# Row halves taken in turn for a state-space mixer's outputs, and four sums of squares that leave for four column quarters together

## The chip, the cores and the metric

The kernel runs on one core of a Trainium2 chip. The metric is the device time of one launch in microseconds (us), as the median of several runs. The kernel before has three: 2160.73, 2167.41 and 2173.29 us, so its median is 2167.41 us.

## The reference, cut to what matters

A trunk of two layers works on 1024 tokens of 1024 channels, in float32. The change lies in layer 0, whose mixer has two branches:

```python
# even_mixer
proj = rms_norm(h, ln) @ w_in
u = proj[..., :512]                         # S5 block: 32 groups of 16 channels
q, k, v = split(proj[..., 512:], 3)         # attention: 8 heads of 64
q = rms_norm(to_heads(q), q_gain)           # mean of 64 squares for each head
k = rms_norm(to_heads(k), k_gain)
# s5_mixer: for each group a complex diagonal recurrence over 64 states
y = einsum(x_r, c_re) - einsum(x_i, c_im) + d * u
y = gelu(y); y = y * sigmoid(y @ w_glu)
```

After it stand stick-breaking attention, an output projection, a squared-ReLU MLP and a gated embedding; layer 1 has a pooling mixer in place of S5 and attention. None of that is touched.

## The kernel before, in words

Activations lie with channels on the 128 partitions and tokens along the free axis, in two halves (`hf`) of 512 tokens. Large products (`gemm`, L477) split both operands into a high and a low part and run three matmuls for each 128 channels. The smaller products of S5, of the norms and of the scores take float32 operands as they are: the trace shows two MATMUL records for each such matmul, and one for each matmul of `gemm`.

**The generators.** `build` writes the work as Python generators, which `weave` interleaves at given rates. Keys, values and queries of a token half come from `kvq`; the four passes of S5 (`s5_pass`, eight of the 32 groups each) are woven into them. What the generators emit is then put into one fixed order for each engine by the framework's scheduler, so a small change in the text can move instructions of other steps too.

**One S5 pass.** Tables of powers are built on DVE and POOL (L319 to L321, L301 to L306). A short product gives the kernel's first taps (L352), which 16 small DMAs lay out as the matrix M (L364). The inputs are transposed (L378, L387) into U. Products of U with VT (L396), whose outputs take the two column halves in turn, give the scan's input. DVE and POOL rotate, scan and rotate back (L400, L408), which yields the states X with real and imaginary part `ri`; the group of an even index has its 64 states on partitions 0 to 63, that of an odd index on 64 to 127. Then come the outputs, the first place of the change: for each group one matmul of U with M over all 128 partitions (L426) and two of X with `ca` over 64 partitions (L428), summed in the same part of a PSUM tile `py`. The four even groups go first, ACT copies their tile out (L431), then the four odd ones. L437 transposes the result back.

**The norms of q and k.** `proj` makes four tiles of 128 channels, two heads each, for a token half, and calls `put_qk` with `j` from 0 to 3. DVE scales the tile (L636), ACT squares it into `sq` (L637), and PE sums the squares of each head with a narrow matmul by `sel` (L638) into rows `32*j` to `32*j+31` of the tile `st`. That is the second place of the change: it comes 16 times, four for each of k and q in each token half. After the fourth, `rsqrt` (L505 to L510, ACT and DVE) makes the reciprocal norms, ACT and DVE split them (L644, L645), four matmuls (L648, the tile `b`) spread them over the heads' rows, and DVE applies them (L650).

**Buffers.** `sq` comes from the tag `t2` (three buffers), which `rsqrt` and `put_v` use too; `acc` (two buffers) holds the input norm's sums and later the two parts at L644. PSUM has two banks each for `z`, `mm` and `b`, one each for `av` and `st`.

Of the kernel before, what the change touches and what calls it, by code (L numbers as in the profile page):

```python
# [19 lines left out]
P = 128  # L20
SEQ = 1024
HT = 512
# [18 lines left out]
class Kern:  # L41
# [282 lines left out]
    def s5_pass(self, gt):  # L324

        nc = self.nc
        v, g = nc.vector, nc.gpsimd
# [12 lines left out]
        ca = self.s5_prod(gt, C2, CS, 0, "ca", g)  # L340
# [5 lines left out]
        for g2 in range(2):  # L346
            rows = slice(64 * g2, 64 * g2 + 64)
            g.tensor_copy(out=self.BD[rows, :, :, 16 * g2:16 * g2 + 16], in_=B2[rows])
        pk = self.p([P, 4, P], "z")
        for m in range(4):  # L350
            for ri in range(2):
                nc.tensor.matmul(pk[0:32, m], self.BD[:, m, ri, :], ca[:, 2 * m + ri].rearrange("p j h -> p (j h)"),  # L352
                                 start=(ri == 0), stop=(ri == 1))
# [5 lines left out]
        M = self.a([P, 8, P], "M")  # L359
# [23 lines left out]
        U = self.a([P, 8, P], "U")  # L383
# [8 lines left out]
        for ri in range(2):  # L392
            pv = self.p([P, 4, P], "z")
            for gl in range(8):
                m, g2 = gl // 2, gl % 2
                nc.tensor.matmul(pv[64 * g2:64 * g2 + 64, m], VT[:, 2 * m + ri, 64 * g2:64 * g2 + 64], U[:, gl],  # L396
                                 start=True, stop=True)
# [13 lines left out]
        X = self.a([P, 2, 4, P], "X")  # L411
        g.memset(X[:, :, :, 0:1], 0.0)
        n = P - 1
        for ri in range(2):
# [3 lines left out]
            tt(v, o, o, b, ALU.subtract if ri == 0 else ALU.add)  # L418
            yield
        yT = self.t([P, 8, 8, 16], "wq", name="yT")  # L420
        for g2 in range(2):
            py = self.p([P, 4, P], "z")
            rows = slice(64 * g2, 64 * g2 + 64)
            for m in range(4):
                gl = 2 * m + g2
                nc.tensor.matmul(py[:, m], U[:, gl], M[:, gl], start=True, stop=False)  # L426
                for ri in range(2):
                    nc.tensor.matmul(py[:, m], X[rows, ri, m, :],  # L428
                                     ca[rows, 2 * m + ri].rearrange("p j h -> p (j h)"),
                                     start=False, stop=(ri == 1))  # L430
            nc.scalar.copy(out=yT[:, :, g2::2, :].rearrange("p t g h -> p g t h"),  # L431
                           in_=py.rearrange("p g (t h) -> p g t h", h=16))
        yield
        for hb in range(2):
            pt = self.p([P, 4, P], "z")
# [193 lines left out]
    def put_qk(self, which, hf, j, ps):  # L629

        nc, v = self.nc, self.nc.vector
        if j == 0:
            self.st = self.p([P, HT], "st")
        sq = self.t([P, HT], "t2", name="sq")
        d = self.qk_dst(which, hf, j)
        v.tensor_tensor(out=d, in0=ps, in1=self.r[hf], op=ALU.mult)  # L636
        nc.scalar.activation(out=sq, in_=d, func=AF.Square)  # L637
        nc.tensor.matmul(self.st[32 * j:32 * j + 32], self.sel, sq, start=True, stop=True)  # L638
        if j == 3:
            r = self.t([P, HT], "t2", name="rq")  # L640
            self.rsqrt(self.st, 64.0, r)

            hi, r4 = (self.t([P, HT], "acc", F32R, name="rq") for _ in range(2))
            nc.scalar.copy(out=hi, in_=r)  # L644
            v.scalar_tensor_tensor(out=r4, in0=hi.bitcast(F32), scalar=self.gain[:, 59:60], in1=r, op0=ALU.mult, op1=ALU.subtract)  # L645
            for i in range(4):
                pb = self.p([P, HT], "b")
                nc.tensor.matmul(pb, self.selT[32 * i:32 * i + 4], r4[32 * i:32 * i + 4], start=True, stop=True)  # L648
                d = self.qk_dst(which, hf, i)
                v.scalar_tensor_tensor(out=d, in0=d, scalar=self.qg[:, which:which + 1], in1=pb, op0=ALU.mult, op1=ALU.mult)  # L650
# [830 lines left out]
```

## Time and profile before

| What | Value |
|---|---|
| Median of three runs | 2167.41 us |
| The profiled execution's own time | 2161.73 us |
| Its span, first to last instruction | 2159.9 us |
| PE busy in the span | 2072.2 us (96%) |
| DVE / ACT / POOL busy | 1838.9 / 1142.2 / 132.1 us |
| Mean granted TensorE clock | 0.98 |
| Projections and S5 | about 0 to 262 us |
| Attention, alone or woven with others | about 262 to 620 us |
| The MLPs, embeddings and pooling | from there to the end |

PE is the engine for matmuls, PEld its weight loads, DVE, ACT and POOL the vector, scalar and general engines. A duration in the table of groups is that of one record from its start to its modelled end. Records on PE overlap, since one starts while the one before it drains, so the time that PE spends on a step is read from start to start in the timeline, and not from durations. The value in brackets behind a row of the timeline is the engine's idle time before it and what ended that.

### The profile page before, as it was taken

The page shows a single profiled execution, that of the slowest core. Times are in us where ns is not written, and L with a number is a line of the kernel's source. Part 1 is how long each engine was busy: PE and PEld are TensorE (multiplying, and loading weights), DVE is VectorE, ACT ScalarE, POOL GpSimd, SP SyncE. Part 2 cuts the span into 40 slices and gives each one's busy share as a digit, 9 for nine tenths or more (in the row PEclk, how much of TensorE's full clock was granted, in tenths as well). Part 3 has the DMA queues.
Part 4 walks back from the last instruction along what each step waited for, and adds up shares of the span by engine and source line. Part 5 has one row for each costly group of instructions (what it writes and reads, how often), then busy time and mean ns, then how long its engine had stood idle before and what let it go on. Part 6 is the DMA issues. An engine that isn't in the chain of part 4 may idle for free.

```text
span 2159.9 us, 24772 instructions
## 1 busy us (share of the span) xinstructions
PE 2072.2 (96%) x9464; PEld 1624.3 (75%) x9464; DVE 1838.9 (85%) x2443; ACT 1142.2 (53%) x1613; POOL 132.1 (6%) x263
## 2 busy tenths in 40 slices
PE   7899999989998999999999999888999999999997
PEld 5676766656577888888888887566888888888886
DVE  8866578978879888998878978999697998879998
ACT  5133466756644563756356555533654656365662
POOL 3856000000000000000000000000000000000000
PEclk9998999989899999999999999998999999999999
DMA  4111111220024112102202122322111201211221
GB/s 151 55 55 55 55 49 32 71 83 30 15 76 138 37 59 69 59 30 78 78 8 71 59 88 69 98 77 99 59 48 41 79 33 56 78 54 34 69 69 59
DMA packets 44742, 136.25 MB, mean 63 GB/s; under 512 B 9552, under 2 KB 10704, under 8 KB 44624
## 3 DMA queue, kind: packets, MB, share of 16 engines
q1 hardware_dynamic: 44624, 134.67, 18.6%
q8 instruction: 74, 1.21, 0.2%
q14 instruction: 44, 0.36, 0.1%
HBM read 129.28 MB, written 4.19 MB: 62 GB/s over the span
## 4 chain that ended last, share of the span: by engine, by line
PE 75%; DVE 19%; ACT 3%; issue 2%; DMA 1%; POOL 0%; SPq 0%; DVEq 0%; ACTq 0%
PE mm L477 27%; PE z L477 15%; PE b L477 12%; PE av L477 6%; PE st L477 6%; DVE rz L698 2%; DVE X L863 2%; DVE w L450 2%; PE z L682 1%; PE av L730 1%; PE b L712 1%; PE z L428 1%; DVE xgl L529 1%; DVE acc L499 1%; DVE na L713 1%
## 5 line engine op out<-in xcount | busy, mean ns | idle before, releaser
L477 PE MATMUL mm<-xgh,w 128*128 128x512 f32 x912 | 300.0, 405 | 15.5 <-ACT w L446 6.2
L450 DVE TENSOR_TENSOR w<-q,w 128x1024 fp32r<-128x1024 f32 x204 | 246.8, 1217 | 0.3 <-ACT w L446 0.3
L446 ACT CAST w<-q 128x1024 fp32r<-128x1024 f32 x204 | 212.8, 1047 | 29.0 <-PE mm L477 14.8
L477 PEld LDWEIGHTS mm<-xgh,w 128*128 128x128 f32 x912 | 173.1, 192 | 62.5 <-issue 9.1
L446 ACT CAST hsh<-H 128x1024 fp32r<-128x1024 f32 x98 | 102.3, 1047 | 197.1 <-PE st L477 88.5
L477 PE MATMUL mm<-xgl,w 128*128 128x512 f32 x456 | 183.0, 401 | 0.0
L446 ACT CAST w<-wr 128x1024 fp32r<-128x1024 f32 x98 | 102.3, 1047 | 150.1 <-PE mm L477 97.9
L477 PE MATMUL z<-xsh,w 128*128 128x512 f32 x576 | 177.7, 390 | 0.0
L863 DVE TENSOR_TENSOR q<-q,q 128x1024 f32<-128x1024 f32 x114 | 137.0, 1219 | 14.0 <-DMA q<-in_w_down 9.5
L450 DVE TENSOR_TENSOR w<-wr,w 128x1024 fp32r<-128x1024 f32 x98 | 128.1, 1312 | 21.1 <-ACT w L446 9.7
L477 PE MATMUL mm<-hsh,w 128*128 128x512 f32 x448 | 137.9, 389 | 0.0
L477 PE MATMUL b<-xsh,w 128*128 128x512 f32 x448 | 137.9, 389 | 0.0
L450 DVE TENSOR_TENSOR hsl<-H,hsh 128x1024 fp32r<-128x1024 f32 x98 | 119.4, 1219 | 11.4 <-ACT hsh L446 11.3
L446 ACT CAST xsh<-X 128x1024 fp32r<-128x1024 f32 x72 | 75.6, 1050 | 98.2 <-PE st L477 51.2
L477 PEld LDWEIGHTS z<-xsh,w 128*128 128x128 f32 x576 | 108.1, 188 | 22.9 <-issue 0.5
L477 PE MATMUL mm<-xsh,w 128*128 128x512 f32 x400 | 123.8, 389 | 0.0
L450 DVE TENSOR_TENSOR xsl<-X,xsh 128x1024 fp32r<-128x1024 f32 x72 | 87.4, 1220 | 38.7 <-ACT xsh L446 38.2
L477 PE MATMUL z<-xsl,w 128*128 128x512 f32 x288 | 112.1, 389 | 0.0
L450 DVE TENSOR_TENSOR xsl<-xt,xsh 128x512 fp32r<-128x512 f32 x108 | 70.1, 685 | 42.5 <-ACT xsh L446 42.5
L477 PEld LDWEIGHTS mm<-xgl,w 128*128 128x128 f32 x456 | 87.9, 193 | 21.8 <-issue 4.1
L477 PE MATMUL b<-hsh,w 128*128 128x512 f32 x336 | 103.6, 389 | 0.0
L477 PE MATMUL z<-hsh,w 128*128 128x512 f32 x336 | 103.4, 389 | 0.0
(360 smaller groups left out, 4874.5 us busy)
## 6 DMA issues: line engine op xcount, KB each, us to landing
q<-in_w_up SPq DMA_DIRECT2D x56, 512.0 KB, 3.6
q<-in_w_down SPq DMA_DIRECT2D x56, 512.0 KB, 3.7
wr<-in_w_in SPq DMA_DIRECT2D x26, 512.0 KB, 3.6
wr<-in_w_out SPq DMA_DIRECT2D x16, 512.0 KB, 3.5
wr<-in_w_up SPq DMA_DIRECT2D x16, 512.0 KB, 3.5
wr<-in_w_down SPq DMA_DIRECT2D x16, 512.0 KB, 3.5
x<-in_x SPq DMA_DIRECT2D x15, 512.0 KB, 5.7
wr<-in_w_gate SPq DMA_DIRECT2D x15, 512.0 KB, 3.5
```

What stands on the lines that cost most here:

```text
L428: nc.tensor.matmul(py[:, m], X[rows, ri, m, :], ca[rows, 2 * m + ri].rearrange("p j h -> p (j h)"), start=False, stop=(ri == 1))
L446: nc.scalar.copy(out=hi, in_=src)
L450: e.tensor_tensor(out=lo, in0=src, in1=hi.bitcast(F32), op=ALU.subtract)
L477: self.nc.tensor.matmul(ps, a, b, start=(first and n == 0 and i == 0), stop=(last and n == K - 1 and i == 2), skip_group_check=going)
L499: e.tensor_tensor(out=self.acc[hf], in0=self.acc[hf], in1=sq, op=ALU.add)
L529: self.nc.vector.scalar_tensor_tensor(out=lo, in0=x, scalar=g, in1=hi.bitcast(F32), op0=ALU.mult, op1=ALU.subtract)
L682: nc.tensor.matmul(pz[:, 0:b1 - b0], self.q[hf][pair // 2][rows, pair % 2, i * P:(i + 1) * P], self.k[b0 // HT][pair // 2][rows, pair % 2, ...
L698: v.tensor_tensor_scan(out=rz[:, rev], data0=na[:, rev], data1=rz[:, rev], initial=0.0, op0=ALU.add, op1=ALU.add)
L712: nc.tensor.transpose(pt[:, (kb - k0) * P:(kb - k0 + 1) * P], zs[:, kb * P:(kb + 1) * P], self.ident)
L713: v.tensor_copy(out=wT[:, k0 * P:k1 * P], in_=pt[:, 0:(k1 - k0) * P])
L730: nc.tensor.matmul(self.avp[64 * o:64 * o + 64, i * P:(i + 1) * P], self.v[kb // 4 * 2 + pair // 2][:, kb % 4, cs], w[:, at * P:(at + 1) * ...
L863: (self.nc.vector if eng == "v" else self.nc.gpsimd).tensor_tensor(out=o, in0=a, in1=b, op=op)
```

## The change

Two places change, and the names of lines shift by two to seven (L426 stays L426, L428 becomes L429, L638 becomes L645, L648 becomes L655, L477 becomes L479).

The outputs of S5 now hold two PSUM tiles at once, one for the even and one for the odd groups. For each `m` the two matmuls by M come first, then the four by X, with even and odd groups in turn. Both copies to `yT` stand behind all of them. In `put_qk`, the squares are kept in a list, the first two in the tag `acc` and the last two in `t2`; the tile `st` is taken at the fourth, and all four matmuls by `sel` are written there, one after the other. No product is added or removed.

```diff
-        for g2 in range(2):
-            py = self.p([P, 4, P], "z")
-            rows = slice(64 * g2, 64 * g2 + 64)
-            for m in range(4):
-                gl = 2 * m + g2
-                nc.tensor.matmul(py[:, m], U[:, gl], M[:, gl], start=True, stop=False)
-                for ri in range(2):
-                    nc.tensor.matmul(py[:, m], X[rows, ri, m, :],
-                                     ca[rows, 2 * m + ri].rearrange("p j h -> p (j h)"),
-                                     start=False, stop=(ri == 1))
+        py = [self.p([P, 4, P], "z") for _ in range(2)]
+        rows = [slice(64 * g2, 64 * g2 + 64) for g2 in range(2)]
+        for m in range(4):
+            for g2 in range(2):
+                nc.tensor.matmul(py[g2][:, m], U[:, 2 * m + g2], M[:, 2 * m + g2], start=True, stop=False)
+            for ri in range(2):
+                for g2 in range(2):
+                    nc.tensor.matmul(py[g2][:, m], X[rows[g2], ri, m, :],
+                                     ca[rows[g2], 2 * m + ri].rearrange("p j h -> p (j h)"),
+                                     start=False, stop=(ri == 1))
+        for g2 in range(2):
             nc.scalar.copy(out=yT[:, :, g2::2, :].rearrange("p t g h -> p g t h"),
-                           in_=py.rearrange("p g (t h) -> p g t h", h=16))
+                           in_=py[g2].rearrange("p g (t h) -> p g t h", h=16))
...
         if j == 0:
-            self.st = self.p([P, HT], "st")
-        sq = self.t([P, HT], "t2", name="sq")
+            self.sqs = []
+        sq = self.t([P, HT], ("acc", "acc", "t2", "t2")[j], name="sq")
...
-        nc.tensor.matmul(self.st[32 * j:32 * j + 32], self.sel, sq, start=True, stop=True)
+        self.sqs.append(sq)
+        if j == 3:
+            self.st = self.p([P, HT], "st")
+            for i, sq in enumerate(self.sqs):
+                nc.tensor.matmul(self.st[32 * i:32 * i + 32], self.sel, sq, start=True, stop=True)
```

The built programs show what stands in PE's row. At the start of the first pass's outputs, PE has before (`z_961` is the PSUM tile of the even groups):

```order
L426 MATMUL z_961<-M_747,U_835 128x128
L428 MATMUL z_961<-ca_670,X_952 128x128 x2
L426 MATMUL z_961<-M_747,U_835 128x128
L428 MATMUL z_961<-ca_670,X_952 128x128 x2
L426 MATMUL z_961<-M_747,U_835 128x128
L638 MATMUL st_817<-sq_948,s5blk_378 32x512
L428 MATMUL z_961<-ca_670,X_952 128x128 x2
```

Now PE has at the same place, with `z_957` for the even and `z_958` for the odd groups:

```order
L426 MATMUL z_957<-M_747,U_833 128x128
L426 MATMUL z_958<-M_747,U_833 128x128
L429 MATMUL z_957<-ca_670,X_948 128x128
L429 MATMUL z_958<-ca_670,X_948 128x128
L429 MATMUL z_957<-ca_670,X_948 128x128
L429 MATMUL z_958<-ca_670,X_948 128x128
L426 MATMUL z_957<-M_747,U_833 128x128
```

Matmuls over 64 partitions and over 128 change places once for each two groups where they did once for each group, and the square of k's third tile no longer stands between them.

The squares of q's first token half, ahead of the third pass's outputs, stand so in PE's row now (`mm_1719` is a projection tile of q, `mm_1792` the first tile of the next keys):

```order
L479 MATMUL mm_1719<-xgl_93,w_1653 128x512
L645 MATMUL st_1753<-sq_1474,s5blk_378 32x512
L645 MATMUL st_1753<-sq_1609,s5blk_378 32x512
L645 MATMUL st_1753<-sq_1682,s5blk_378 32x512
L479 MATMUL mm_1792<-xgh_291,w_1721 128x512
L479 MATMUL mm_1792<-xgh_291,w_1722 128x512
L479 MATMUL mm_1792<-xgl_292,w_1721 128x512
L645 MATMUL st_1753<-sq_1750,s5blk_378 32x512
```

Three squares stand side by side, and the scheduler has put three matmuls of a projection ahead of the fourth. In the other three groups it is three and one as well, with other work between them. Before, the four stood 25 to 58 PE instructions apart.

In the third pass's outputs PE has before, around the matmuls that spread q's norms (L648, then L655):

```order
L426 MATMUL z_1829<-M_1562,U_1641 128x128
L638 MATMUL st_1823<-sq_1824,s5blk_378 32x512
L428 MATMUL z_1829<-ca_1485,X_1782 128x128
L648 MATMUL b_1770<-rq_1767,selT 128x512
L648 MATMUL b_1773<-rq_1767,selT 128x512
L428 MATMUL z_1829<-ca_1485,X_1782 128x128
```

And now:

```order
L429 MATMUL z_1828<-ca_1483,X_1782 128x128
L426 MATMUL z_1827<-M_1560,U_1638 128x128
L655 MATMUL b_1770<-rq_1767,selT 128x512
L655 MATMUL b_1773<-rq_1767,selT 128x512
L426 MATMUL z_1828<-M_1560,U_1638 128x128
L429 MATMUL z_1827<-ca_1483,X_1782 128x128
```

Thirteen of the pass's 24 output matmuls stand ahead of the first of these now, and eleven did before; between the last square and it, 21 projection matmuls stand where 17 did, and no square where one did. Behind attention's start the scheduler has put rows of all engines into another order, through 27 of attention's 48 units; PE, DVE and ACT have as many instructions as before.

## The prediction, made before the changed kernel ran

> **What bounds the kernel now.** I read the page first, then the busy times by stretch, then the chain of waits in the stretch where the change lies, and last the timeline of PE there. The page gives the engines' shares and the chain of the whole span:
>
> ```profile
> PE 2072.2 (96%) x9464; PEld 1624.3 (75%) x9464; DVE 1838.9 (85%) x2443; ACT 1142.2 (53%) x1613; POOL 132.1 (6%) x263
> PE 75%; DVE 19%; ACT 3%; issue 2%; DMA 1%; POOL 0%; SPq 0%; DVEq 0%; ACTq 0%
> ```
>
> The changed steps run from about 77 to 331 us. By stretch (busy us of PE, PEld, DVE, ACT and POOL, then PE's clock):
>
> ```profile
> 140.00:180.00 40.00, 38.63 (x203) 29.67 (x202) 24.04 (x28) 12.36 (x19) 29.40 (x58) 1.00 0.17 53
> 180.00:220.00 40.00, 37.96 (x167) 26.85 (x166) 30.34 (x37) 10.71 (x15) 22.32 (x48) 0.83 0.16 53
> 220.00:260.00 40.00, 38.66 (x217) 28.20 (x216) 21.54 (x34) 13.74 (x20) 4.21 (x2) 1.00 0.25 74
> 300.00:340.00 40.00, 37.28 (x192) 23.86 (x191) 32.05 (x49) 25.22 (x43) 0.00 (x0) 1.00 0.16 54
> 345.00:620.00 275.00, 260.38 (x1384) 170.65 (x1385) 244.52 (x319) 177.14 (x260) 0.00 (x0) 0.94 0.13 44
> ```
>
> PE is busy for 95 to 97% of them, and no other engine comes near before attention. In attention DVE has 89% as well. The chain from 60 to 262 us:
>
> ```profile
> by line: PE mm L477 29.3%; PE z L428 10.1%; DVE S L408 5.9%; PE z L426 5.7%; DVE W L400 5.1%; PE z L396 4.1%; PE st L638 3.7%; issue 3.6%; POOL W L400 2.9%; PE z L352 2.8%; DVE s5blk L211 2.6%; DVE w L450 2.5%; PE b L648 2.4%; PE z L387 2.0
> ```
>
> The three changed lines hold 19.5% of it, 39 of 202 us. So PE time saved here is mostly time saved, except where PE then waits for S5's scan (S, W) or for the norm's chain.
>
> **Part 1, S5's outputs.** Rows of the timeline from the first pass, each merging the records of one step:
>
> ```profile
> 102.64 0.71 PE L428 MATMUL z<-ca,X 64*128 64x128 f32 x4
> 103.28 0.49 PE L426 MATMUL z<-M,U 128*128 128x128 f32 x2
> 103.70 0.71 PE L428 MATMUL z<-ca,X 64*128 64x128 f32 x4
> 104.34 0.49 PE L426 MATMUL z<-M,U 128*128 128x128 f32 x2
> ```
>
> From start to start, a group's matmul by M (two records) takes 0.42 us and its two by X (four records) 0.64: 1.06 us a group. Two more records of a kind cost 0.64 - 0.42 = 0.22 us; the other 0.20 of the first pair is paid whenever the kind changes. What two row halves cost in turn is shown by attention's scores (L682), which run two heads in turn in the first token half and one alone in the second:
>
> ```profile
> 286.14 0.49 PE L682 MATMUL z<-k,q 64*128 64x128 f32 x4
> 286.56 0.28 PE L686 MATMUL z<-maskb,identb 128*128 128x128 bf16 x2
> 345.98 0.48 PE L682 MATMUL z<-k,q 64*128 64x128 f32 x2
> 346.39 1.09 PE L730 MATMUL av<-na,v 128*64 128x128 f32 x14
> ```
>
> Four records of two heads take 0.42 us, two of one head 0.41: the second head is free. So for two groups the new order costs 0.42 + 0.22 for M and 0.42 + 0.22 for X, 1.28 us in place of 2.12. Sixteen such pairs save 13.4 us. If the halves did not overlap, X would cost 0.42 + 3 x 0.22 = 1.08, and only the fewer changes of kind would be saved: 0.40 x 16 = 6.4 us.
>
> **Part 2, the squares.**
>
> ```profile
> 91.57 0.39 PE L477 MATMUL mm<-xgh,w 128*128 128x512 f32 x1
> 92.11 1.04 PE L638 MATMUL st<-sq,s5blk 128*32 128x512 f32 x2
> 93.08 0.50 PE L477 MATMUL mm<-xgh,w 128*128 128x512 f32 x1
> 93.42 0.39 PE L477 MATMUL mm<-xgl,w 128*128 128x512 f32 x1
> 93.65 0.62 PE L477 MATMUL mm<-xgh,w 128*128 128x512 f32 x2
> ...
> 100.61 1.05 PE L638 MATMUL st<-sq,s5blk 128*32 128x512 f32 x2
> 101.59 0.71 PE L428 MATMUL z<-ca,X 64*128 64x128 f32 x4
> ```
>
> A projection matmul takes 0.23 us (93.42 to 93.65). Between 91.57 and 93.42 stand two of these and a square, so the square costs 1.85 - 0.46 = 1.39 us, of which 0.97 is its own and the rest the change of kind on both sides. Where it stood between a matmul by M and one by X (100.61 to 101.59), which change kind anyway, it cost 0.98. I take 1.2, about the middle. Column tiles in turn are shown by L396, whose outputs take two column halves:
>
> ```profile
> 237.13 2.02 PE L396 MATMUL z<-U,VT 128*64 128x128 f32 x32
> 239.08 0.50 PE L477 MATMUL mm<-xgl,w 128*128 128x512 f32 x1
> ```
>
> Its 32 records take 1.95 us, 0.12 for each pair, where one record alone takes 0.11. So column tiles side by side should also cost one. In the built program three of each four squares stand side by side and the fourth apart. That hides two of four, 8 in all: 9.6 us, with bounds 8 x 0.98 = 7.8 and 8 x 1.39 = 11.1 us. If they did not overlap, only about 8 x 0.3 = 2.4 us of changes of kind would go.
>
> The Trainium skill (TensorE: Matmul & The Clock Gate, Part 3: Packing small matmuls) gives 2.38 times for three column tiles of 512, not three. By that, three squares would take 1.22 in place of 0.97 us, and the sum would be 1.0 us smaller. The trace has two column tiles at nearly twice the rate, and none with three or four.
>
> PE also waits for the squares now:
>
> ```profile
> PE st L638 <- ACT sq L637: 7.4, 6, 3.3
> 80.12 0.57 ACT L381 COPY uT<-z 128x512 f32<-128x512 f32 x1
> 80.26 1.05 PE L638 MATMUL st<-sq,s5blk 128*32 128x512 f32 x2 [3.25 <-ACT sq L637]
> 81.24 1.57 PE L387 MATMUL z<-ident,uT 128*128 128x128 f32 x8
> ```
>
> Most of the longest one is not won: L387, next in PE's row, reads the copy that ACT ends at 80.69, so only 0.5 us goes. Of the other 4.1 us I count half, since the next step may be late too. That makes 2.5 us (bounds 0.5 and 7.4).
>
> **Part 3, what is late next.** Three things take some back.
>
> First, the scan. The first outputs by X wait for it in two passes:
>
> ```profile
> 98.12 1.08 PE L428 MATMUL z<-ca,X 64*128 64x128 f32 x4 [0.67 <-DVE X L400]
> 251.54 0.49 PE L428 MATMUL z<-ca,X 64*128 64x128 f32 x4 [0.86 <-DVE X L400]
> ```
>
> In the first pass a square no longer lies ahead of this wait, so its 1.2 us comes back as waiting. In the last pass four squares now lie there where one did, but four projection matmuls have moved ahead of it; I count 0.5. Together 1.7 us.
>
> Second, the norm's chain in the third pass:
>
> ```profile
> 192.51 1.05 PE L638 MATMUL st<-sq,s5blk 128*32 128x512 f32 x2
> 201.91 1.04 PE L638 MATMUL st<-sq,s5blk 128*32 128x512 f32 x2 [0.88 <-ACT sq L637]
> 202.73 1.75 DVE L645 SCALAR_TENSOR_TENSOR rq<-rq,gain,rq 128x512 fp32r<-128x512 f32 x1
> 204.54 0.79 PE L648 MATMUL b<-rq,selT 4*128 4x512 f32 x2 [1.16 <-DVE rq L645]
> ```
>
> From the first square's end (192.51 + 0.97) to the first L648 it takes 11.1 us. PE has 21 projection matmuls (4.8 us) and thirteen outputs (2 x 1.28 + 0.3) to do meanwhile now, 7.7 us, so it would stand for 3.4 us behind L648, with the pass's last eleven outputs queued. It waits 2 us in that stretch today (L648's 1.16, and 0.88 for a square). The longer wait costs 1.4 us, and the cheaper outputs ahead of it win nothing beyond the four projection matmuls that moved there: I take 2 us off. DVE's row of that stretch is unchanged; on ACT the next keys' first `sq` now needs a buffer that L645 reads, and the copies of L431 are behind it, but those ended later than L645 anyway.
>
> Third, the copies to `yT`:
>
> ```profile
> 206.08 0.58 ACT L431 COPY yT<-z 128x512 f32<-128x512 f32 x1 [4.22 <-PE z L428]
> ```
>
> Before, the first of the two was behind the second half's matmuls; now both follow the last one, 1.2 us ahead of L437. Five projection matmuls (1.15 us) cover them in three passes and 24 in the first. I count 0.3 us in three passes, 0.9 in all.
>
> **The sum:** 13.4 + 9.6 + 2.5 - 1.7 - 2.0 - 0.9 = 20.9 us, on an execution of 2161.73 (span 2159.9, 1.8 around it). Such an execution would take 2140.8 us. It lay 5.7 below the median of 2167.41; against that median I predict 2146.5 us, 1.0% less.
>
> **The rivals.**
>
> *The scan binds.* If S5's chain through ACT, DVE and POOL, and not PE, sets each pass, PE's new idle time stays inside the passes. For it speak the two waits above and POOL's 29.4 of 40 us; against it, those waits are 0.67 and 0.86 us in 50. Then only what lies outside the scans is won: the squares of attention's stretch (2 x 1.2), four of the passes' (4.8), less the copies, some 6 us: about 2161 us.
>
> *No overlap.* If the tiles don't run together, 6.4 + 2.4 + 2.5 - 4.6 = 6.7 us remain: about 2161 us. L682 and L396 speak against it.
>
> *The clock.* PE ran at half clock here:
>
> ```profile
> 204.58:218.23 13.65, 13.65 (x40) 9.60 (x41) 9.54 (x9) 2.19 (x4) 11.13 (x40) 0.50 0.07 28
> ```
>
> This costs 6.8 us, and starts where PE waits for L648. If the new order avoids it, about 2140 us; if it comes again, its outputs are saved at the double price, which balances a longer wait. The Trainium skill (TensorE: Matmul & The Clock Gate, Part 1: The HAM clock gate) states half clock after an idle window of about 3.4 us; 13.65 us is four of those, and my wait of 3.4 us would be just such a window.
>
> *Slower: attention in its new order.* From 345 to 620 us DVE is busy for 89% and PE for 95%, and 27 of 48 units stand in another order. Today PE waits for weights in four places there:
>
> ```profile
> PE b L712 <- ACT zs L703: 6.8, 4, 3.4
> ```
>
> If each of the 27 units' L712 now waited the mean of these, 1.7 us more, 46 us would be lost and 25 net: about 2192 us. It decides from 0.8 us a unit on, where the 20.9 are eaten. Against it, ACT and DVE have the same work, and start it earlier.
>
> **How the numbers follow.** The forecast has 0.60, the scan 0.13, no overlap 0.07, the clock 0.10, attention 0.10. About 0.5% (11 us) is what a measurement of this kernel can tell from no change. Under 2156.6 us lie 0.56 of the forecast, the clock's 0.10 and 0.03 of the scan's: faster 0.69. Slower takes 0.08 of attention's 0.10. The same is left with 0.23. The range's low end has every upper bound (13.4 + 11.1 + 7.4 + 6.8 - 1.7 - 0.9 = 36 us): 2131. Its high end has the weakest rivals' 6 us and one more half-clock stretch of 6.8: 2168.
>
> **What would show it.** Right: X's outputs in pairs that start together, a pair of groups in 1.28 us, three squares in about 1.0, no wait of PE for ACT's `sq`, a longer one for L645's `rq`. Wrong: records of the two halves one behind the other; waits for X of over 3 us a pass; attention's stretch longer by more than a few us.

## The result, and the profile after

The changed kernel takes 2147.38 us, median of four runs (2147.02 to 2148.42). The kernel before took 2170.35 us on the same chip (2160.73 to 2177.27). The ratio is 0.9911, 95% interval 0.9886 to 0.9936: the whole interval lies below 1, so the kernel is faster, by some 0.9%. A second comparison gave 2149.44 against 2165.53 us, ratio 0.9916 (0.9891 to 0.9940). So the gain is 16 to 23 us between medians. The profiled execution took 2147.02 us (span 2145.2), 14.7 less than the profiled one before.

The chain by engine and the stretches of the page, as they were shown for the kernel before:

```profile
PE 2054.4 (96%) x9464; PEld 1614.4 (75%) x9464; DVE 1843.8 (86%) x2443; ACT 1141.0 (53%) x1613; POOL 133.7 (6%) x263
PE 73%; DVE 20%; ACT 3%; issue 2%; DMA 1%; POOL 1%; SPq 0%; DVEq 0%; ACTq 0%; POOLq 0%
```

```profile
140.00:180.00 40.00, 37.98 (x232) 30.49 (x232) 28.51 (x32) 13.49 (x21) 30.46 (x58) 1.00 0.21 68
180.00:220.00 40.00, 36.41 (x186) 26.50 (x183) 32.73 (x39) 12.70 (x19) 22.34 (x48) 0.87 0.22 74
220.00:260.00 40.00, 39.09 (x227) 28.52 (x226) 22.74 (x34) 19.07 (x27) 3.92 (x2) 1.00 0.18 53
...
345.00:620.00 275.00, 261.20 (x1375) 172.55 (x1374) 240.79 (x307) 171.86 (x246) 0.00 (x0) 0.94 0.15 51
```

PE is busy for 17.8 us less in the span. In the first two stretches it stands idle for 2.0 and 3.6 us of 40, where it was 1.4 and 2.0 before, and DVE's busy time there has risen from 24.0 to 28.5 and from 30.3 to 32.7. The chain from 60 to 252 us, which ends with S5's last pass, shows the same shift by line:

```profile
by line: PE mm L479 22.1%; DVE W L400 7.9%; DVE S L408 7.7%; PE z L429 7.1%; issue 6.8%; PE z L426 5.1%; DVE w L452 4.3%; POOL W L400 3.9%; PE z L352 2.9%; DVE s5blk L211 2.8%; PE b L655 2.5%; DVE X L400 2.5%; ACT w L448 1.9%; PE z L396 1.6
```

The outputs (L426 with L428, now L429) have fallen from 15.8 to 12.2% of it, and the squares (3.7% before) have left the part of the list that is shown. The scan on DVE, W and S, has risen from 11.0 to 15.6%, and X has joined with 2.5.

What the change does to PE is as it was meant. First the outputs, on PE's timeline of the second pass, then three squares together and the fourth alone:

```profile
153.05 0.71 PE L429 MATMUL z<-ca,X 64*128 64x128 f32 x8
153.70 0.71 PE L426 MATMUL z<-M,U 128*128 128x128 f32 x4
154.34 0.71 PE L429 MATMUL z<-ca,X 64*128 64x128 f32 x8
...
112.83 1.06 PE L645 MATMUL st<-sq,s5blk 128*32 128x512 f32 x6
113.82 0.77 PE L439 MATMUL z<-ident,yT 128*128 128x128 f32 x5
114.51 1.04 PE L645 MATMUL st<-sq,s5blk 128*32 128x512 f32 x2
115.49 0.55 PE L439 MATMUL z<-ident,yT 128*128 128x128 f32 x3
```

A pair of groups takes 154.34 - 153.05 = 1.29 us. Six records of three squares take 0.99 us, as long as the two of the single square behind (0.98).

Where the time went is read from the first start of a few steps in PE's timeline (us; the kernel before, the changed one, and a second profile of the changed one):

| Step | before | after | difference | after, again |
|---|---|---|---|---|
| first pass, first output by M | 97.1 | 93.4 | -3.7 | 93.9 |
| first pass, transposes of yT | 113.1 | 113.8 | +0.7 | 115.6 |
| second pass, first output | 148.6 | 149.8 | +1.1 | 151.0 |
| third pass, first output | 197.5 | 194.2 | -3.3 | 195.5 |
| third pass, transposes of yT | 217.1 | 210.4 | -6.7 | 211.7 |
| fourth pass, first output | 244.0 | 235.2 | -8.8 | 237.4 |
| fourth pass, last transpose of yT | 262.1 | 251.7 | -10.4 | 255.4 |
| first matmul of the output projection of S5's half | 391.8 | 382.3 | -9.5 | 385.8 |
| first matmul of the MLP | 612.8 | 598.2 | -14.7 | 602.4 |
| span | 2159.9 | 2145.2 | -14.7 | 2148.8 |

The first pass wins nothing. PE's timeline there, with the wait and what follows it:

```profile
93.37 0.60 PE L426 MATMUL z<-M,U 128*128 128x128 f32 x4
98.13 1.40 PE L429 MATMUL z<-ca,X 64*128 64x128 f32 x8 [4.15 <-DVE X L400]
99.46 1.22 PE L426 MATMUL z<-M,U 128*128 128x128 f32 x4
...
105.22 1.23 PE L429 MATMUL z<-ca,X 64*128 64x128 f32 x8
106.38 1.22 PE L479 MATMUL mm<-xgh,w 128*128 128x512 f32 x2
```

PE comes 3.7 us earlier and then waits 4.15 us for X, where it waited 0.67. On DVE, the last rotations of X start at the same time in both kernels, first before, then after:

```profile
97.38 1.29 DVE L400 TENSOR_TENSOR X<-X,W 128x508 f32<-128x508 f32 x2 [1.17 <-POOL W L400]
```

```profile
97.39 1.28 DVE L400 TENSOR_TENSOR X<-X,W 128x508 f32<-128x508 f32 x2 [1.15 <-POOL W L400]
```

Then the outputs run at half clock. From 98.13 to 106.38 they take 8.25 us, where the seven steps at the second pass's pace would take 7 x 0.645 = 4.5. The stretches of half clock in the first and third pass (the clock stands third from the end):

```profile
97.86:108.10 10.24, 9.97 (x48) 8.02 (x49) 8.42 (x10) 1.70 (x3) 10.24 (x18) 0.50 0.15 52
200.26:210.50 10.24, 9.75 (x32) 6.50 (x33) 6.74 (x6) 2.65 (x4) 10.24 (x39) 0.50 0.12 49
```

The first is new. The second has taken the place of the 13.65 us at 204.58. It begins at the wait for the norm of the third pass:

```profile
196.68 0.49 PE L426 MATMUL z<-M,U 128*128 128x128 f32 x2
200.75 0.80 PE L655 MATMUL b<-rq,selT 4*128 4x512 f32 x2 [3.59 <-DVE rq L652]
```

### The profile page after: what moved, and what is told of

Read it like the earlier page. It is cut to its first block, busy times and chain, and to the rows that moved or that the text cites. A ratio compares the mean times of both kernels' runs of the same rounds, so it can differ in the third digit from the quotient of the medians.

```text
span 2145.2 us, 24774 instructions
## 1 busy us (share of the span) xinstructions
PE 2054.4 (96%) x9464; PEld 1614.4 (75%) x9464; DVE 1843.8 (86%) x2443; ACT 1141.0 (53%) x1613; POOL 133.7 (6%) x263
## 4 chain that ended last, share of the span: by engine, by line
PE 73%; DVE 20%; ACT 3%; issue 2%; DMA 1%; POOL 1%; SPq 0%; DVEq 0%; ACTq 0%; POOLq 0%
PE mm L479 26%; PE z L479 15%; PE b L479 12%; PE av L479 6%; PE st L479 6%; DVE rz L705 2%; DVE w L452 2%; DVE X L870 2%; PE z L689 1%; PE av L737 1%; PE b L719 1%; DVE xgl L531 1%; DVE acc L501 1%; DVE na L720 1%; DVE W L400 1%
## 5 line engine op out<-in xcount | busy, mean ns | idle before, releaser
L479 PE MATMUL mm<-xgh,w 128*128 128x512 f32 x912 | 300.7, 407 | 15.5 <-ACT w L448 6.2
L479 PEld LDWEIGHTS mm<-xgh,w 128*128 128x128 f32 x912 | 174.1, 194 | 62.8 <-ACT w L448 8.6
L479 PE MATMUL mm<-xgl,w 128*128 128x512 f32 x456 | 183.5, 402 | 0.0
L479 PE MATMUL z<-xsh,w 128*128 128x512 f32 x576 | 177.7, 390 | 0.0
L479 PE MATMUL b<-xsh,w 128*128 128x512 f32 x448 | 137.9, 389 | 0.0
L479 PE MATMUL mm<-hsh,w 128*128 128x512 f32 x448 | 137.9, 389 | 0.0
L479 PEld LDWEIGHTS z<-xsh,w 128*128 128x128 f32 x576 | 108.1, 188 | 22.8 <-issue 0.5
L479 PE MATMUL mm<-xsh,w 128*128 128x512 f32 x400 | 123.8, 389 | 0.0
L479 PE MATMUL z<-xsl,w 128*128 128x512 f32 x288 | 112.1, 389 | 0.0
L479 PE MATMUL b<-hsh,w 128*128 128x512 f32 x336 | 103.6, 389 | 0.0
L479 PEld LDWEIGHTS mm<-xgl,w 128*128 128x128 f32 x456 | 88.2, 193 | 20.4 <-issue 2.4
L479 PE MATMUL z<-hsh,w 128*128 128x512 f32 x336 | 103.4, 389 | 0.0
```

The costliest lines, as they stand in the source:

```text
L479: self.nc.tensor.matmul(ps, a, b, start=(first and n == 0 and i == 0), stop=(last and n == K - 1 and i == 2), skip_group_check=going)
```

## The experiments

The theory after the first look: PE's saving is real, the scan and the norm's chain give part of it back as waits, and a long wait brings a stretch of half clock. The rivals: the tiles overlap less than the records suggest; or the waits are incidental, and can be edited away. "X wait" is PE's in the first pass, "rq wait" PE's for the norm.

**One part at a time.** First the new outputs with the old squares:

```diff
-        if j == 3:
-            self.st = self.p([P, HT], "st")
-            for i, sq in enumerate(self.sqs):
-                nc.tensor.matmul(self.st[32 * i:32 * i + 32], self.sel, sq, ...)
+        nc.tensor.matmul(self.st[32 * j:32 * j + 32], self.sel, sq, start=True, stop=True)
```

> The outputs of S5 as in the change, the squares as before. Overlap theory: a pair of groups costs 1.28 us in place of 2.12 wherever the clock is full, so PE saves up to 13.4 us; but the saving before a wait for X or for L645's rq comes back as waiting, so 8 to 12 us are won against the median of before, about 2159 us, and PE still waits about 7 us for ACT's sq. Theory that only fewer changes of kind count: at most 6 us, 2164 us or more.

Measured: 2156.07 us, ratio 0.9951 (0.9934 to 0.9968). PE's timeline of it, around the first pass:

```profile
98.34 1.09 PE L429 MATMUL z<-ca,X 64*128 64x128 f32 x8 [0.43 <-DVE X L400]
...
122.49 0.50 PE L650 MATMUL b<-rq,selT 4*128 4x512 f32 x2 [2.69 <-DVE rq L647]
```

With squares ahead of the outputs the X wait is short and the outputs run at full clock. They end earlier, and PE then waits 2.69 us for the norm.

Then the new squares with the old outputs (the diff of `put_qk` alone).

> The squares as in the change, the outputs of S5 as before. Overlap theory: three squares side by side in about 1.0 us, 9.6 us saved and the waits for sq gone, less the longer waits for X; about 9 us won, 2161 us. This and the run with the outputs alone should together give about what the whole change gives, 23 us between medians. Rival (the gain is the new order of attention, which both parts shuffle in their own way): the two do not add up.

Measured: 2169.22 us, ratio 1.0006 (0.9991 to 1.0021): nothing won. The X wait is followed by half clock here too, for 17 us, over outputs that are longer:

```profile
98.76 1.39 PE L428 MATMUL z<-ca,X 64*128 64x128 f32 x4 [2.90 <-DVE X L400]
100.81 1.22 PE L428 MATMUL z<-ca,X 64*128 64x128 f32 x4
```

So the parts don't add: about 10 us and none alone (against the 2165.97 us of before in that comparison), 16 to 23 together. The rival written down with this kernel, attention's new order, is not why. In the profiles, the last transpose of yT comes 6.9 us earlier than before with the outputs alone, 9.3 later with the squares alone and 10.4 earlier with both; behind it 0.9, 3.5 and 4.3 us are won, which nearly add. What doesn't add lies within S5's passes.

**Without the turn.** Each group's two matmuls by X stay together, even group first; everything else is as in the changed kernel.

```diff
-            for ri in range(2):
-                for g2 in range(2):
+            for g2 in range(2):
+                for ri in range(2):
                     nc.tensor.matmul(py[g2][:, m], X[rows[g2], ri, m, :],
```

> As changed, but of the four matmuls by X of a pair both of the even group stand ahead of both of the odd one; changes of kind, waits and all else as in the change. Overlap theory: X costs 1.08 us a pair in place of 0.64 at full clock, less what the one neighbouring pair of records of the two halves still overlaps; 16 x 0.44 = 7 us of PE time, of which some 2 us hide in the wait for L645's rq: 2151 to 2155 us. Theory that only fewer changes of kind count: 2147 us, no change.

Measured: 2150.05 us, ratio 0.9924 (0.9898 to 0.9951), which the intervals don't tell apart from the changed kernel. The timeline of its second pass says why:

```profile
152.50 0.71 PE L426 MATMUL z<-M,U 128*128 128x128 f32 x4
153.14 0.72 PE L429 MATMUL z<-ca,X 64*128 64x128 f32 x8
153.79 0.71 PE L426 MATMUL z<-M,U 128*128 128x128 f32 x4
```

A pair of groups still takes 1.29 us. The eight records start in pairs, 13 ns apart (7 ns in the changed kernel). No record says which group it belongs to, but the two halves must be running side by side, since eight records of both take 0.65 us, as four of one took 0.64 before, although the even group's four are issued ahead of those of the odd one. So the experiment didn't take the overlap away. What it shows is that the turn isn't needed: it is enough here that the two halves' matmuls stand next to each other, with none over all rows between.

**Filling the X wait.** Four useless matmuls of 512 columns go into a free bank between the first M and X of the first pass; the output isn't touched.

```diff
+            if gt == 0 and m == 0:
+                pad = self.p([P, HT], "av")
+                for _ in range(4):
+                    nc.tensor.matmul(pad, U[:, 0], M[:, 0:4], start=True, stop=True)
```

> As changed, with four useless matmuls of 512 columns (U by M into the free bank av, about 0.9 us each) between the first pass's first matmuls by M and by X, where PE waits 4.15 us for X; the output is not touched by them. Theory that the half-clock stretch of 10.2 us at 97.9 us comes from that wait: the stretch goes, the first pass's outputs take 1.28 us a pair in place of 2.31, and 4 to 5 us are won although work was added: about 2142.5 us. Rival (the stretch has another cause, such as the float32 outputs themselves): it stays, 2147 us or a little over.

Measured: 2150.62 us, ratio 0.9926 (0.9898 to 0.9955). The half clock at 98 us is gone; the clock is 1.00 from 97 to 104 us. But the time is no shorter than the changed kernel's. A little later PE stands again, and a stretch of half clock follows there:

```profile
93.72 3.60 PE L430 MATMUL av<-M,U 128*128 128x512 f32 x8
...
121.35 0.79 PE L659 MATMUL b<-rq,selT 4*128 4x512 f32 x2 [3.71 <-DVE rq L656]
122.07 2.34 PE L352 MATMUL z<-ca,s5blk 128*32 128x128 f32 x10
```

```profile
121.29:131.53 10.24, 10.18 (x38) 7.35 (x39) 6.19 (x9) 2.39 (x5) 4.82 (x11) 0.50 0.06 12
```

So the theory was right on what brought the first pass's half clock, and wrong on what its removal is worth: a wait and a stretch of 10.24 us come back at the norm. The rq wait is explained by DVE's timeline, with POOL's behind it:

```profile
113.78 0.69 DVE L514 SCALAR_TENSOR_TENSOR ra<-st,ra 128x512 f32<-128x512 f32 x1 [2.94 <-ACT ra L513]
114.50 4.63 DVE L515 TENSOR_SCALAR ra<-ra 128x512 f32<-128x512 f32 x1
119.17 0.69 DVE L516 TENSOR_TENSOR rq<-rq,ra 128x512 f32<-128x512 f32 x1
```

```profile
118.11 0.73 POOL L306 TENSOR_TENSOR tab<-tab,tt 128x256 f32<-128x256 f32 x1
```

L515 took 4.63 us. In the changed kernel the median of this step's 16 is 0.43. It ends at 119.13, just behind POOL's row of small steps for the next pass's tables (118.84).

**Moving the waits away.** Three kernels try to schedule around them. The first issues the first pass's outputs later:

```diff
+        for _ in range(3 if gt == 0 else 0):
+            yield
         yT = self.t([P, 8, 8, 16], "wq", name="yT")
...
-        weave(steps(kv, 20), s5, 2.6)
+        weave(steps(kv, 20), s5, 2.75)
```

> Three turns more of the weave ahead of the first pass's outputs, and the weave's rate 2.75 in place of 2.6, so that in the first pass the outputs come after all of the third tile's matmuls and after three of the squares; the later passes as in the changed kernel. If the wait for X (4.15 us) is what brings the half clock at 97.9 us, both go: the outputs take 5.1 us, not 9.2, and the wait is 0, and as the outputs now lie between the squares and the spread of rq they also cover the norm's chain, so nothing else comes late: 4.15 + 4.1, about 2139. If a wait merely moves on to the next chain (rq), as in the padded kernel, a PE wait of over 3 us shows up before 130 us, and the time is that of the changed kernel, 2147 to 2151.

Measured: 2149.1 us, ratio 0.9926 (0.9898 to 0.9955): no better than the changed kernel. The X wait went, one step of 3.41 us is left of the half clock there, and the transposes of yT came at 111.0 in place of 113.8 us; but a wait for weights (2.52 us) stands ahead of the squares, and the third pass waits for rq as before:

```profile
94.99 0.50 PE L481 MATMUL mm<-xgh,w 128*128 128x512 f32 x1 [2.52 <-DVE w L454]
...
198.78 0.69 PE L657 MATMUL b<-rq,selT 4*128 4x512 f32 x2 [4.02 <-DVE rq L654]
```

The second kernel issues the spread of rq after the next tile's projection:

```diff
-            for i in range(4):
-                pb = self.p([P, HT], "b")
+            def spread(): ...          # the same loop
+            if which == 0 and hf == 1:
+                spread()
+            else:
+                self.pending = spread  # run in proj at j == 1, ahead of put
```

> The four matmuls that spread rq, and their multiplies, are issued after the next tile's projection and not right behind the norm (but for the last queries). The first pass keeps its wait for X and its half clock. In the third pass the 3.75 us that PE waits for rq amid the outputs should go, and with it the half clock at 200.3 us, which stretched 10 us of outputs and projection by about 4 us: 2147.4 - 3.75 - 4, about 2140. If something else (X, or another chain) is due at the same time, the wait shows under another name and the time is 2146 to 2150.

Measured: 2158.31 us, ratio 0.9962 (0.9944 to 0.9980), 9 to 11 us over the changed kernel's two medians. PE now waits 4.8 us for the buffers of the spread, since DVE, which must empty them, stands itself:

```profile
DVE w L452 <- POOL tt L304: 9.3, 1, 9.3
```

The third has both edits.

> Both edits: outputs of the first pass later, spread later. If each wait and its half clock is its own term, they add: 2147.4 - 8 - 8, about 2132. If the scan and the norm trade the same time to and fro, about the better of the two alone, 2139 or more.

Measured: 2148.0 us, ratio 0.9912 (0.9886 to 0.9939). S5 ends 5.3 us earlier than in the changed kernel (246.4 us), and the MLP starts 0.9 us later (599.1). The worst wait on PE, and DVE behind it:

```profile
212.18 0.79 PE L661 MATMUL b<-rq,selT 4*128 4x512 f32 x1 [6.42 <-DVE q L663]
```

```profile
208.45 2.41 DVE L454 TENSOR_TENSOR w<-wr,w 128x1024 fp32r<-128x1024 f32 x1 [9.25 <-POOL tt L304]
```

**Four squares together.** The third with the last square ordered ahead of the other three:

```diff
-            for i, sq in enumerate(self.sqs):
-                nc.tensor.matmul(...)
+            first = None
+            for i in (3, 0, 1, 2):
+                mm = nc.tensor.matmul(self.st[32 * i:32 * i + 32], self.sel, self.sqs[i], ...)
+                self.order(mm, first)
+                first = first or mm
```

> As both, and the square of the last tile is put ahead of the other three, so that all four are issued next to each other. The trace of the changed kernel has 0.99 us for three squares side by side and 0.97 us for the fourth alone. If the four quarters of the columns do work at once, four take 1.0 us and 8 norms save 8 x 0.97 = 7.8 us less what is hidden in waits: 4 to 8 us below the kernel with both edits, 2124 to 2128. If the fourth waits for ACT, PE now stands for it with the three behind it, and the gain is below 2 us.

Measured: 2144.47 us, ratio 0.9903 (0.9874 to 0.9932), 3.5 us below the kernel without it; their intervals don't part them. The expectation counted 8 norms, but the changed place has four (16 squares), so about 4 x 0.97 = 3.9 us were to be won. Four squares take 102.69 - 101.69 = 1.00 us:

```profile
101.69 1.06 PE L651 MATMUL st<-sq,s5blk 128*32 128x512 f32 x8
102.69 0.49 PE L428 MATMUL z<-M,U 128*128 128x128 f32 x2
```

So four quarters overlap as three do. Whether the 3.9 us were won stays open: between the medians lie 3.5, between the two profiles' spans 0.7, and PE still waits 4.9 us for rq in this one.

**Two controls.** The kernel before and the changed one once more, word for word.

> The kernel before, word for word: what a difference of nothing looks like. Ratio 1.000 within 0.003. If the half-clock stretches are set by the kernel's own waits, they lie at the same places as in the first trace (a long one at about 204 us, none between 90 and 110 us) to within a few us; if chance sets them, their places and lengths change and the span with them, by some 5 us.

Measured: ratio 0.9995 (0.9976 to 1.0014), span 2159.6 us. The long half-clock stretch of the third pass is there again, 13.65 us at 204.3, and none lies between 90 and 110 us.

> The changed kernel, word for word, beside the others on one chip. 2145 to 2149. If the wait for X brings the half clock in the first pass, both are there again: a PE wait of 3 to 4.5 us at about 94 us, and a stretch of 10 us or so that begins at 95 to 100 us; and the same behind the wait for rq at 197 us.

Measured: 2149.44 us, span 2148.8. Both waits return:

```profile
PE z L429 <- DVE X L400: 5.0, 2, 4.1
PE b L655 <- DVE rq L652: 3.6, 1, 3.6
```

So do both stretches, at 97.5 and 199.9 us, each 13.65 us long in place of 10.24. The waits are the kernel's own, not chance; how many steps of 3.41 us the half clock lasts varies between executions. The spans of these two differ by 3.6 us.

**A shorter chain for rq.** The rounded copy is made on DVE.

```diff
-            nc.scalar.copy(out=hi, in_=r)
+            v.tensor_copy(out=hi, in_=r)
```

> The rounded copy of the norm's root is made on DVE and not on ACT (the trace of the changed kernel has it at 0.62 us on ACT), so the multiply behind it needs no trip to ACT and back, and on DVE stands ahead of the 1.6 us of splitting a weight. The wait for rq at 197 us should fall from 3.75 us to about 2.6. If waits of under 3 us don't bring the half clock, the stretch at 200 us goes too and with it some 4 us: about 2142. If they do, 1 us is left, less 4 copies on DVE: 2146 to 2148.

Measured: 2145.97 us, ratio 0.9902 (0.9881 to 0.9924). The rq wait is 3.8 us, no shorter, and the half clock stays (13.65 us at 199). On DVE the new copy takes 1.37 us there, where ACT took 0.62, with POOL's step beside it:

```profile
196.10 1.43 DVE L512 TENSOR_TENSOR rq<-rq,ra 128x512 f32<-128x512 f32 x1
197.56 1.37 DVE L651 CAST rq<-rq 128x512 fp32r<-128x512 f32 x1
...
199.45 1.15 DVE L652 SCALAR_TENSOR_TENSOR rq<-rq,gain,rq 128x512 fp32r<-128x512 f32 x1
```

```profile
196.94 3.11 POOL L321 TENSOR_TENSOR ca<-ca,cat 128x512 f32<-128x512 f32 x2
```

The median is 3.5 us below the changed kernel's of the same comparison, less than the intervals of the ratios can part. But five of these six runs (2145.47 to 2146.15 us, one of 2148.06) are shorter than the shortest of the changed kernel's six beside them (2146.48), so a small gain is likely. The mechanism meant for it did not occur, and what brought it is open.

**All that seemed to help, together:** later outputs, four squares, and the copy on DVE, with the spread in its old place.

> Later outputs in the first pass, the four squares side by side, and the rounded copy on DVE, with the spread where the changed kernel has it. Of the kernel with later outputs, spread later and four squares (2144.5) the one harm was the 5 us that PE stood behind DVE's weight split; without it, and with a rq wait of about 2.6 us in the third pass, 2139 to 2141. If DVE's stream of the third pass sets when rq is done whatever PE gains ahead of it, the wait for rq there is 4 us or more, and the time 2144 to 2147.

Measured: 2155.42 us, ratio 0.9948 (0.9927 to 0.9969), worse than the changed kernel on the same chip, 2149.44 us (the shortest run here took 2151.15 us, the longest there 2151.76). The profile is of the longest of its eight runs, 2161.64 us. In it the first pass is won: its transposes start at 108.2 us. Then one step of DVE takes 7.04 us where the median of its eight is 0.68, to just behind the end of POOL's last table step at 120.0, and PE waits behind it, with half clock from 119.24 to 126.07:

```profile
113.51 7.04 DVE L321 TENSOR_TENSOR vs<-vs,vst 128x512 f32<-128x512 f32 x1
```

```profile
119.28 0.72 POOL L306 TENSOR_TENSOR tab<-tab,tt 128x256 f32<-128x256 f32 x1
```

```profile
121.41 1.12 PE L670 MATMUL b<-ident,vT 128*128 128x128 f32 x4 [4.64 <-DVE vT L667]
```

The second pass's products with VT start at 139.7 us, 6.0 later than in the kernel before, and the lead is gone. By the intervals no version tried is shown to beat the changed kernel; the shorter chain alone looks a little faster, by its runs.

## Why the prediction was right or wrong

**Part 1** held where the clock was full: 1.29 us a pair against 1.28 predicted, from attention's scores; without overlap it would have been 1.72. The reason given, that the halves go in turn, was too narrow, as the kernel without the turn showed.

**Part 2** held: three squares in 0.99 us, four in 1.00, so the trace's own column tiles were the better guide than the Trainium skill's 2.38 times for three tiles (TensorE: Matmul & The Clock Gate, Part 3: Packing small matmuls), by which three would take 1.22 us. PE's own waits for `sq`, 7.4 us before, are gone; its weight loads wait 0.8 us for it where they waited 12.2.

**Part 3, the scan**, is the step that was mis-sized. It was put at 1.7 us, 1.2 of it in the first pass, because one square lay ahead of the wait. But X is done when the scan is done, and that did not move at all (97.38 and 97.39 us above). Everything that PE saves ahead of it comes back, 3.5 us more waiting, and the wait then brought half clock over the outputs, 8.25 - 4.5 = 3.7 us. That is 7.2 us in place of 1.2, and so that pass kept nothing of its outputs and squares. The scan rival was right for this pass, and wrong for the third and fourth, which together gained 9.3 us (from -1.1 at the third pass's first L352 to -10.4 at the end).

**Part 3, the norm of the third pass:** PE's wait was put at 3.4 us and is 3.59. The reason for its length was not seen. In the traces of before and after, DVE's steps ahead of rq take two to three times as long as elsewhere, and POOL's 128x512 steps (L320, L321) run beside them. In the changed kernel:

```profile
194.07 1.28 DVE L511 TENSOR_SCALAR ra<-ra 128x512 f32<-128x512 f32 x1
```

Its median is 0.43 us.

**The clock rival.** Half clock was not avoided: the third pass has it in every kernel run here, and a new stretch came in the first. The Trainium skill's rule of an idle window of about 3.4 us (TensorE: Matmul & The Clock Gate, Part 1: The HAM clock gate) fits in part. In six profiles PE waits 2.6 to 4.2 us for X in the first pass, and each has 10 to 17 us of half clock from 97 to 99 us on; of the eight without that wait none has more than one step of 3.41 us there. But a wait of 2.69 us for rq had none behind it, and the third pass of the kernel before got 13.65 us behind waits of 0.88 and 1.16. That a long wait brings the half clock is thus shown for the first pass, by filling it; what else brings it, and how long it stays, is not.

**Attention's new order** did not hurt. From the end of S5 to the MLP the changed kernel is 4.3 us faster (3.7 in the second pair). How much of it the squares that stand there won is not settled: the steps have another order, and the lead swings on the way, as the row at 391.8 us shows with 9.5.

**The sum.** 20.9 us were predicted between two profiles; 14.7 and 10.8 came in two pairs of them. The scan's term, 6.0 us too small by the rows above, is as much as nearly all of the 6.2 missing in the first pair, but the other terms were not measured one by one, and the second pair was not taken apart. That the median was met to 1 us is luck: the profiled execution of before lay near the short end of its runs (2160 to 2177), while those of the changed kernel lie close together. Subtracting from a median what was worked out on one execution was the weak joint. The runs show what goes with the scatter of before: in the 18 that stood beside the single parts, the mean granted clock falls from 0.978 at 2161.01 us to 0.970 at 2177.06, so the longer runs have more half clock. Why was not tested.

## What to carry to other kernels

Work saved on the busiest engine is kept only behind the last thing that it waits for: before counting a saving, find when the operand of the next wait is ready, and whether that moves. In this kernel every schedule that went around one wait led to the next; look for steps that take several times their median, and for what runs beside them. As far as these traces go, products on two row halves need only be neighbours to overlap, and up to four column quarters go at the price of one.

## What the runs showed of the hardware

- Column quarters: three squares 0.99 us, four 1.00, one 0.98, each of 512 columns in float32.
- Row halves overlap even if four records of one half are issued ahead of the other's: records start in pairs 13 ns apart, against 7 in turn, and a pair of groups takes 1.29 us either way.
- DVE next to POOL. In each of the first three passes of the kernel before and of the changed one, one DVE step took 4.5 to 6.1 us, where its median is 1.2 to 1.6, while POOL ran its row of small table steps, and ended 0.5 to 1.6 us behind that row. In other kernels it fell on other steps: 4.63 us in place of 0.43 (the kernel that fills the X wait), 7.04 in place of 0.68 (the last kernel). Beside POOL's 128x512 steps, steps of DVE took 1.15 to 1.43 us (rows of the kernel with the shorter chain) in place of 0.4 to 0.75. The Trainium skill (SBUF — State Buffer, Who interferes with whom) states that a DVE step with two SBUF inputs, or one in a 2-port mode, contends with POOL's reads for a shared pair of ports that one of them holds alone; the rows agree, though none shows in which mode a step ran. No kernel moved POOL's work, so that this is the cause is argued from the rows, not shown by taking it away.
- The two long stretches of half clock in S5's passes began at the same places to 0.5 us in two profiles of the changed kernel, but lasted 10.24 us in one and 13.65 in the other.
